# Gate and up products of a transformer block's FFN with the weights as stationary operand

## The chip, the cores and the metric

The kernel runs on one core of a Trainium2 chip. The core has five engines that run side by side and meet at semaphores: TensorE (matrix products), VectorE, ScalarE, GpSimd and SyncE, which issues most of the DMAs. The profile calls them PE, DVE, ACT, POOL and SP, and shows TensorE's weight loads apart from its matmuls, as PEld. The metric is the time of one execution on the device in microseconds, and lower is better. The time before is the median of three runs, 1760.88 us (1760.65 to 1761.78).

## The reference

One block: a mixer of four branches, then an FFN, for 256 tokens of width 2048 in fp32. The change is in the FFN, which is 5632 wide:

```python
def swiglu(h, w_g, w_u, w_d):
    return (jax.nn.silu(h @ w_g) * (h @ w_u)) @ w_d
...
x = x + g1 * merge_branches(h, branches, w_gate[i], w_branch, w_o[i])
x = x + g2 * swiglu(modulate(rms_norm(x, norm2_w[i]), sh2, sc2),
                    w_ffn_gate[i], w_ffn_up[i], w_ffn_down[i])
```

`h` is 256 x 2048, `w_g` and `w_u` are 2048 x 5632, `w_d` is 5632 x 2048.

## The kernel before

A TensorE matmul has a stationary operand (`lhsT`, loaded into the array first, up to 128 columns) and a moving one (`rhs`, streamed through it, up to 512 columns). It sums over the 128 partitions and writes into a bank of PSUM, with one row for each stationary column and one column for each moving one.

**Products in three parts.** Large products are made in the type fp32r. Each fp32 operand is split into a rounded part `hi` and a rest `lo`, and `hi*hi + hi*lo + lo*hi` are summed in PSUM. For weights, `split` (line 76) has ScalarE copy the piece to `hi` (line 94) and VectorE subtract (line 95). Three buffers each of `hi` and `lo` go round. For activations `tsplit` does the same (lines 137 and 138).

**`gemm`** makes 256 tokens by 512 columns of a product. It goes through the contraction in pieces of two k-tiles of 128 rows: one DMA of 512 KB on SyncE's queue, one split, and then for each k-tile and each half `t` of the tokens three matmuls (`mm3`, lines 98 to 101). The activations are stationary (128 features x 128 tokens) and the weights moving (128 x 512), so a PSUM bank holds 128 tokens x 512 columns. With 16 k-tiles (`KT`) that is 16 x 2 x 3 = 96 matmuls. The pools give four PSUM banks to products (`acc`) and four to transposes and small results (`tr`).

**The FFN** (from line 915) goes over eleven groups of 512 columns. For group `n` the gate product goes into `fg` tiles, ScalarE writes its silu to `m` (`mid` in the profile, line 921), the up product goes into `fu` tiles, and VectorE multiplies it into `m` (line 925). `m` has tokens on its partitions. The down product needs features there, so TensorE transposes `m` in eight blocks of 128 x 128, as plain fp32 matmuls with the identity (line 933, `m_tp`), and `tsplit` makes `mh` and `ml` from PSUM. The lists of these, `mT`, are the stationary operand of the down product (`dn` tiles), four groups of 512 columns with 44 k-tiles each, which ends the kernel.

**Order.** Within an engine, instructions run in the order in which they are issued. A scheduler makes that order from the program and its dependencies. It places the transposes of a group a few matmuls into the gate product of the next one, and the last group's into the beginning of the down product. Beside all this, jobs taken from a list (`pump`) accumulate the block's other modulation vectors on VectorE (`macc`) until about the middle of the FFN.

Of the kernel before, what the change touches and what calls it, by code (L numbers as in the profile page):

```python
# [9 lines left out]
F32R = mybir.dt.float32r  # L10
# [5 lines left out]
P = 128  # L16
D = 2048
S = 256
NT = S // P
KT = D // P  # L20
# [26 lines left out]
def block_kernel(ctx: ExitStack, tc: tile.TileContext, t_in, out):  # L47
    nc = tc.nc
# [10 lines left out]
    def U(name, dtype=F32):  # L59
        return up.tile([P, 1024], dtype, tag="u", name=name, bufs=NU)  # L60
# [4 lines left out]
    def acc_ps(name):  # L65
        return psa.tile([P, 512], F32, tag="acc", name=name)

    def tr_ps(name):
        return pst.tile([P, 512], F32, tag="tr", name=name)


    def raw_tile(name):
        return wp.tile([P, 1024], F32, tag="raw", name=name, bufs=NRAW)
# [4 lines left out]
    def split(src, name, shape, roomy=False):  # L78

        n = 1  # L80
        for s_ in shape:
            n *= s_
        assert n <= 1024
        if roomy:
            hi, lo = U(name + "h", F32R), U(name + "l", F32R)
        else:
            hi = wp.tile([P, 1024], F32R, tag="hi", name=name + "h", bufs=3)
            lo = wp.tile([P, 1024], F32R, tag="lo", name=name + "l", bufs=3)
        if len(shape) == 2:
            hv = hi[:, :n].rearrange("p (a b) -> p a b", a=shape[0])  # L90
            lv = lo[:, :n].rearrange("p (a b) -> p a b", a=shape[0])
        else:
            hv, lv = hi[:, :n], lo[:, :n]
        state["act"] = nc.scalar.copy(hv, src)  # L94
        state["dve"] = nc.vector.tensor_tensor(lv, src, hv.bitcast(F32), ALU.subtract)  # L95
        return hv, lv

    def mm3(ps, xh, xl, wh, wl, first, last):
        nc.tensor.matmul(ps, lhsT=xh, rhs=wh, start=first, stop=False)  # L99
        nc.tensor.matmul(ps, lhsT=xh, rhs=wl, start=False, stop=False)  # L100
        state["pe"] = nc.tensor.matmul(ps, lhsT=xl, rhs=wh, start=False, stop=last)  # L101

    def gemm(xT, w, row0, nk, col0, name, tail=1, inside=()):

        pieces = []
        ps = [acc_ps(f"{name}_ps{t}") for t in range(NT)]
        for k0 in range(0, nk, 2):  # L110
            raw = raw_tile(f"{name}_w{k0}")
            rv = raw.rearrange("p (k f) -> p k f", k=2)
            r = row0 + k0 * P
            nc.sync.dma_start(
                rv, w[r:r + 2 * P, col0:col0 + 512].rearrange("(k p) f -> p k f", p=P))
            pump()
            wh, wl = split(rv, f"{name}_{k0}", (2, 512), k0 + 2 * tail >= nk and tail > 1)
            pieces += [(k0 + j, wh[:, j, :], wl[:, j, :]) for j in range(2)]
            next_step()
            if k0 == 4:  # L120
                for do in inside:
                    do()
            if k0 + 2 * tail < nk:
                tiles = [(p_, t) for p_ in pieces for t in range(NT)]
                pieces = []
            elif k0 == nk - 2:
                tiles = [(p_, t) for t in range(NT) for p_ in pieces]
            else:
                continue
            for (kt, h_, l_), t in tiles:  # L130
                xh, xl = xT(kt)
                sl = slice(t * P, (t + 1) * P)
                mm3(ps[t], xh[:, sl], xl[:, sl], h_, l_, kt == 0, kt == nk - 1)
        return ps

    def tsplit(hi, lo, src):
        nc.scalar.copy(hi, src)
        nc.vector.tensor_tensor(lo, src, hi.bitcast(F32), ALU.subtract)
# [5 lines left out]
    state = {"tick": 0, "hold": True}  # L144
# [6 lines left out]
    def pump():  # L151
        state["tick"] += 3
        if state["tick"] >= 5:
            state["tick"] -= 5
            if jobs and not state["hold"]:
                jobs.pop(0)()

    def next_step():
        if steps:
            steps.pop(0)()  # L160
# [16 lines left out]
    ident = const.tile([P, P], F32, name="ident")  # L177
# [598 lines left out]
    for i in range(1, len(CHUNKS) - 1):  # L776
        nk = CHUNKS[i]
# [76 lines left out]
    for n in range(4):  # L854
        while n == 2 and 4 not in col2:
            jobs.pop(0)()
        state["hold"] = n > 1
        ps = gemm(lambda kt: (yT[kt // 4][0][:, kt % 4, :], yT[kt // 4][1][:, kt % 4, :]),
                  t_in["w_o"], 0, KT, n * 512, f"wo{n}", tail=WO_TAIL if n == 3 else 1,
                  inside=wo_later)  # L860
        wo_later = []
        gsl = gbc[2][n // 2][:, (n % 2) * 512:(n % 2) * 512 + 512]
        tmps = U(f"tmp{n}")
        for t in range(NT):
            if n == 3:

                wo_last.append((ps[t], gsl, tmps))
                continue
            wo_later.append(lambda a=(n, t, ps[t], gsl, tmps): residual(*a))
# [7 lines left out]
    def norm2(t):  # L877
        added = residual(3, t, *wo_last[t])
        nc.vector.tensor_reduce(ss2[:, t:t + 1], ssq[:, t, :], AX.X, ALU.add)
        rstd_of(ss2[:, t:t + 1], rs2[:, t:t + 1], 1, 1.0 / D)  # L880
        sl = slice(t * P, (t + 1) * P)
        xns = []
        for q in range(4):
            xn = U(f"xn2_{q}{t}")
            xns.append(xn)
            if q % 2 == 0:
                nc.scalar.activation(xn[:, :512], xres[q][:, t, :], AF.Copy, scale=rs2[:, t:t + 1])
            else:
                nc.vector.tensor_scalar(xn[:, :512], xres[q][:, t, :], rs2[:, t:t + 1], None, ALU.mult)
        for q in range(4):  # L890
            xn, hf = xns[q][:, :512], xns[q][:, 512:]
            ps = tr_ps(f"h2_tp{q}{t}")
            for b in range(4):
                nc.tensor.transpose(ps[:, b * P:(b + 1) * P], xn[:, b * P:(b + 1) * P], ident)
            for b in range(4):
                kt = q * 4 + b
                bs = slice(b * P, (b + 1) * P)
                if b % 2 == 0:
                    nc.vector.tensor_scalar(hf[:, bs], ps[:, bs], a2[:, kt:kt + 1],
                                            col2[3][:, kt:kt + 1], ALU.mult, ALU.add)  # L900
                else:
                    nc.scalar.activation(hf[:, bs], ps[:, bs], AF.Identity, scale=a2[:, kt:kt + 1],
                                         bias=col2[3][:, kt:kt + 1])
            tsplit(h2[q][0][:, :, sl], h2[q][1][:, :, sl], hf.rearrange("p (k t) -> p k t", k=4))
        return added

    with tc.high_priority(offset=NORM2_AHEAD):
        added = norm2(0)
# [5 lines left out]

    mT = []
    for n in range(FF // 512):
        with tc.issue_after(added.ins) if n == 0 else nullcontext():
            pg = gemm(h2x, t_in["w_ffn_gate"], 0, KT, n * 512, f"fg{n}")
        m = U(f"mid{n}").rearrange("p (t f) -> p t f", t=NT)
        for t in range(NT):  # L920
            nc.scalar.activation(m[:, t, :], pg[t], AF.Silu)
        state["hold"] = False
        pu = gemm(h2x, t_in["w_ffn_up"], 0, KT, n * 512, f"fu{n}")
        for t in range(NT):
            nc.vector.tensor_tensor(m[:, t, :], m[:, t, :], pu[t], ALU.mult)
        mh = U(f"mh{n}", F32R).rearrange("p (k t) -> p k t", k=4)
        ml = U(f"ml{n}", F32R).rearrange("p (k t) -> p k t", k=4)
        for pr in range(2):
            ps = tr_ps(f"m_tp{n}{pr}")
            for j in range(2):  # L930
                for t in range(NT):
                    b = pr * 2 + j
                    nc.tensor.transpose(ps[:, (j * 2 + t) * P:(j * 2 + t + 1) * P],
                                        m[:, t, b * P:(b + 1) * P], ident)
            tsplit(mh[:, 2 * pr:2 * pr + 2, :], ml[:, 2 * pr:2 * pr + 2, :],
                   ps.rearrange("p (k t) -> p k t", k=2))
        mT.append((mh, ml))

    while jobs:
# [1 line left out]
    for n in range(4):  # L941
        ps = gemm(lambda kt: (mT[kt // 4][0][:, kt % 4, :], mT[kt // 4][1][:, kt % 4, :]),
                  t_in["w_ffn_down"], 0, FF // P, n * 512, f"dn{n}")
# [78 lines left out]
```

## Time and profile before

The profile shows one execution, with all its instructions on a time axis that starts at the first one.

| | us |
|---|---|
| median of three runs | 1760.88 |
| the profiled execution, on the device | 1761.78 |
| its span on the profile's axis | 1759.7 |
| gate product of group 0 begins | 1019.5 |
| gate product of group 1 begins | 1067.0 |
| down product begins | 1514.0 |

TensorE's matmuls are pipelined, so their spans overlap; how fast it goes is read from the distance of starts. A group row of the profile gives line, engine, operation, output and inputs by the program's names with buffer numbers left out, shapes, count, then busy time, mean ns of one, and the engine's idle time before them with what ended it. In shapes, `128*128 128x512` is a stationary operand of 128 x 128 and a moving one of 128 x 512. Both fp32 and fp32r stand as f32 there: the matmuls of lines 99 to 101 are fp32r, those with `ident`, `s_ps` (attention scores, line 556) and `o_ps` (attention output, line 588) are plain fp32.

### The profile page before, as it was taken

To read this page: it belongs to the slowest core of one execution; us is meant where nothing else is said; L and a number is where in the kernel's file an instruction comes from. 1 tells how busy PE (TensorE), PEld (TensorE's weight loads), DVE (VectorE), ACT (ScalarE), POOL (GpSimd) and SP (SyncE) were. 2 spreads that over 40 slices of the span, in tenths; PEclk is the share of its full clock that TensorE was granted. 3 is DMA by queue.
4 is the path that set the end of the run, shared out by engine and by line. 5 is a ranking of instruction groups with operands and counts; after the bars stand their busy time and mean duration, and the time that the engine had idled before them with its cause. 6 is when DMAs were issued, how large, how long until landed. Compare 5 with 4: busy or idle time off the path is not lost.

```text
span 1759.7 us, 20840 instructions
## 1 busy us (share of the span) xinstructions
PE 1733.2 (98%) x7874; PEld 1396.4 (79%) x7874; DVE 1135.6 (65%) x1302; ACT 742.3 (42%) x874; POOL 56.0 (3%) x74
## 2 busy tenths in 40 slices
PE   6999999999999999999999999999999999999998
PEld 3677777878888888888888878888888888888887
DVE  5875655676588777787878777775554444544554
ACT  5322322344555554444344564445444443433332
POOL 1000000102002000000000000000000000000000
PEclk9999999999999999999999999999999999999999
DMA  9676575446468777999999759875666556565663
GB/s 332 248 287 227 190 250 173 145 124 194 158 200 286 239 247 261 308 306 308 321 323 300 267 172 304 298 252 180 191 189 187 188 190 191 191 202 193 207 206 113
DMA packets 182537, 402.60 MB, mean 229 GB/s; under 512 B 12771, under 2 KB 14997, under 8 KB 182437
## 3 DMA queue, kind: packets, MB, share of 16 engines
q1 hardware_dynamic: 180036, 396.11, 68.0%
q0 software_dynamic: 1248, 3.06, 0.6%
q10 hardware_dynamic: 1152, 2.10, 0.3%
q8 instruction: 62, 1.02, 0.2%
q14 instruction: 39, 0.31, 0.1%
HBM read 399.12 MB, written 2.10 MB: 228 GB/s over the span
## 4 chain that ended last, share of the span: by engine, by line
PE 96%; DMA 1%; DVE 1%; issue 1%; ACT 0%; SPq 0%; POOL 0%; POOLq 0%; DVEq 0%; ACTq 0%
PE gt_ps L100 7%; PE gt_ps L101 7%; PE gt_ps L99 7%; PE in_psx L99 5%; PE in_psx L100 5%; PE fu_ps L100 5%; PE fu_ps L99 5%; PE fu_ps L101 5%; PE in_psx L101 5%; PE dn_ps L101 5%; PE dn_ps L100 5%; PE dn_ps L99 5%; PE fg_ps L99 4%; PE fg_ps L101 4%; PE fg_ps L100 4%; PE br_ps L100 2%
## 5 line engine op out<-in xcount | busy, mean ns | idle before, releaser
L404 DVE SCALAR_TENSOR_TENSOR macc<-mod,cs,macc 128x1024 f32<-128x1024 f32 x128 | 164.0, 1283 | 0.0
L318 DVE TENSOR_TENSOR in_x<-in_x,in_psx 128x512 f32<-128x512 f32 x110 | 74.3, 685 | 45.6 <-PE in_psx L101 45.1
L94 ACT CAST in_2h<-in_w 128x1024 fp32r<-128x1024 f32 x33 | 34.7, 1051 | 160.5 <-PE in_psc L101 91.9
L99 PE MATMUL in_psx<-in_0h,hxh 128*128 128x512 f32 x220 | 90.0, 416 | 1.3 <-ACT hxh L298 1.0
L94 ACT CAST in_0h<-in_w 128x1024 fp32r<-128x1024 f32 (+1 forms) x56 | 57.7, 1035 | 73.0 <-PE in_psx L101 29.1
L100 PE MATMUL in_psx<-in_0l,hxh 128*128 128x512 f32 x220 | 87.2, 399 | 0.0
L101 PE MATMUL in_psx<-in_0h,hxl 128*128 128x512 f32 x220 | 86.3, 395 | 0.0
L95 DVE TENSOR_TENSOR in_0l<-in_w,in_0h 128x1024 fp32r<-128x1024 f32 (+1 forms) x56 | 67.3, 1201 | 3.2 <-ACT in_0h L94 3.2
L95 DVE TENSOR_TENSOR in_2l<-in_w,in_2h 128x1024 fp32r<-128x1024 f32 x33 | 40.4, 1225 | 40.0 <-ACT in_2h L94 40.0
L99 PEld LDWEIGHTS in_psx<-in_0h,hxh 128*128 128x128 f32 x220 | 41.4, 190 | 25.0 <-issue 7.4
L100 PE MATMUL in_psx<-in_2l,hxh 128*128 128x512 f32 x132 | 51.8, 392 | 0.0
L99 PE MATMUL in_psx<-in_2h,hxh 128*128 128x512 f32 x132 | 51.5, 391 | 0.0
L101 PE MATMUL in_psx<-in_2h,hxl 128*128 128x512 f32 x132 | 51.5, 390 | 0.0
L100 PEld LDWEIGHTS in_psx<-in_0l,hxh 128*128 128x128 f32 x220 | 42.1, 191 | 10.8 <-issue 1.9
L101 PEld LDWEIGHTS in_psx<-in_0h,hxl 128*128 128x128 f32 x220 | 41.9, 190 | 9.0
L318 DVE TENSOR_TENSOR in_c<-in_c,in_psc 128x512 f32<-128x512 f32 x40 | 27.2, 686 | 28.6 <-PE in_psc L101 28.5
L226 PE MATMUL mod_ps<-mod_w,cst 128*32 128x512 f32 (+1 forms) x288 | 41.1, 591 | 2.9 <-DMA mod_w<-in_mod 2.8
L95 DVE TENSOR_TENSOR gt_12l<-gt_w,gt_12h 128x1024 fp32r<-128x1024 f32 x16 | 19.6, 1225 | 19.3 <-ACT gt_12h L94 19.3
L99 PE MATMUL in_psc<-in_0h,hch 128*128 128x512 f32 x80 | 31.5, 396 | 0.0
L100 PE MATMUL in_psc<-in_0l,hch 128*128 128x512 f32 x80 | 31.2, 390 | 0.0
L101 PE MATMUL in_psc<-in_0h,hcl 128*128 128x512 f32 x80 | 31.2, 390 | 0.0
L100 PEld LDWEIGHTS in_psx<-in_2l,hxh 128*128 128x128 f32 x132 | 24.8, 188 | 6.0 <-DVE hcl L301 0.8
(659 smaller groups left out, 5132.5 us busy)
## 6 DMA issues: line engine op xcount, KB each, us to landing
mod<-in_w_mod SPq DMA_DIRECT2D x128, 512.0 KB, 5.4
gt_w<-in_w_gate SPq DMA_DIRECT2D x128, 512.0 KB, 5.3
fg_w<-in_w_ffn_gate SPq DMA_DIRECT2D x88, 512.0 KB, 3.6
fu_w<-in_w_ffn_up SPq DMA_DIRECT2D x88, 512.0 KB, 3.6
dn_w<-in_w_ffn_down SPq DMA_DIRECT2D x88, 512.0 KB, 3.8
in_w<-in_w_in SPq DMA_DIRECT2D x87, 512.0 KB, 4.6
mod_w<-in_mod SPq DMA_DIRECT2D x64, 512.0 KB, 5.8
wo_w<-in_w_o SPq DMA_DIRECT2D x32, 512.0 KB, 5.4
```

The source lines that it names most:

```text
L94: state["act"] = nc.scalar.copy(hv, src)
L95: state["dve"] = nc.vector.tensor_tensor(lv, src, hv.bitcast(F32), ALU.subtract)
L99: nc.tensor.matmul(ps, lhsT=xh, rhs=wh, start=first, stop=False)
L100: nc.tensor.matmul(ps, lhsT=xh, rhs=wl, start=False, stop=False)
L101: state["pe"] = nc.tensor.matmul(ps, lhsT=xl, rhs=wh, start=False, stop=last)
L226: nc.tensor.matmul(ps[32 * j:32 * j + 32, :2 * nf], lhsT=cst[:, kk, :], rhs=rvs[j // kn][:, j % kn, :, :].rearrange("p s f -> p (s f)"), s ...
L318: nc.vector.tensor_tensor(dst, dst, ps, ALU.add)
L404: nc.vector.scalar_tensor_tensor(macc[m][h_], mod_raw.pop((m, kk, h_)), cs[:, 0, kk:kk + 1], macc[m][h_], ALU.mult, ALU.add)
```

## The change

A new function `gemm_t` makes the same 256 tokens by 512 columns with the operands' roles swapped: a 128 x 128 block of weights is stationary, and all 256 tokens move. For each k-tile and each of the four blocks `b` of 128 columns there are three matmuls, so 16 x 4 x 3 = 192 in a product. A result has features on its partitions, and two blocks share a PSUM bank: bank 0 holds columns 0 to 255, bank 1 columns 256 to 511, each as two halves of 256 tokens. DMAs, splits and `pump` are as in `gemm`.

In groups 1 to 10 the gate and up products use it. Their `m` then has features on the partitions, so the transposes go, and `tsplit` reads `m` itself in SBUF in place of a transpose's bank. Group 0 stays as it was.

```diff
+    def gemm_t(xT, w, nk, col0, name):
+        ps = [acc_ps(f"{name}_ps{i}") for i in range(2)]
+        for k0 in range(0, nk, 2):
...
+            wh, wl = split(rv, f"{name}_{k0}", (2, 512))
+            next_step()
+            for j in range(2):
+                kt = k0 + j
+                xh, xl = xT(kt)
+                for b in range(4):
+                    sl = slice(b * P, (b + 1) * P)
+                    o = ps[b // 2][:, (b % 2) * S:(b % 2 + 1) * S]
+                    nc.tensor.matmul(o, lhsT=wh[:, j, sl], rhs=xh,
+                                     start=kt == 0 and b % 2 == 0, stop=False)
+                    nc.tensor.matmul(o, lhsT=wh[:, j, sl], rhs=xl, start=False, stop=False)
+                    state["pe"] = nc.tensor.matmul(o, lhsT=wl[:, j, sl], rhs=xh, start=False,
+                                                   stop=kt == nk - 1 and b % 2 == 1)
+        return ps
...
     for n in range(FF // 512):
-        with tc.issue_after(added.ins) if n == 0 else nullcontext():
-            pg = gemm(h2x, t_in["w_ffn_gate"], 0, KT, n * 512, f"fg{n}")
...
+        if n == 0:
+            with tc.issue_after(added.ins):
+                pg = gemm(h2x, t_in["w_ffn_gate"], 0, KT, n * 512, f"fg{n}")
+        else:
+            pg = gemm_t(h2x, t_in["w_ffn_gate"], KT, n * 512, f"fg{n}")
...
         for pr in range(2):
-            ps = tr_ps(f"m_tp{n}{pr}")
-            for j in range(2):
-                for t in range(NT):
-                    b = pr * 2 + j
-                    nc.tensor.transpose(ps[:, (j * 2 + t) * P:(j * 2 + t + 1) * P],
-                                        m[:, t, b * P:(b + 1) * P], ident)
+            if n == 0:
+                src = tr_ps(f"m_tp{n}{pr}")
...
+            else:
+                src = m[:, pr, :]
             tsplit(mh[:, 2 * pr:2 * pr + 2, :], ml[:, 2 * pr:2 * pr + 2, :],
-                   ps.rearrange("p (k t) -> p k t", k=2))
+                   src.rearrange("p (k t) -> p k t", k=2))
```

The up product is switched in the same way as the gate product.

The first place where the order shows it is TensorE's, at the end of group 1's up product (`fu1`) and the start of group 2's gate product (`fg2`). Before, a row being line, operation, output and inputs, and the moving operand's shape:

```order
L101 MATMUL fu1_ps1_8697<-fu1_14h_8841,h2l3_8087 128x512
L99 MATMUL fg2_ps0_8875<-fg2_0h_8879,h2h0_8080 128x512
L100 MATMUL fg2_ps0_8875<-fg2_0l_8880,h2h0_8080 128x512
L933 MATMUL m_tp10_8861<-ident_85,mid1_8693 128x128
L933 MATMUL m_tp11_8868<-ident_85,mid1_8693 128x128
L101 MATMUL fg2_ps0_8875<-fg2_0h_8879,h2l0_8081 128x512
L99 MATMUL fg2_ps1_8876<-fg2_0h_8879,h2h0_8080 128x512
L933 MATMUL m_tp10_8861<-ident_85,mid1_8693 128x128 x3
L933 MATMUL m_tp11_8868<-ident_85,mid1_8693 128x128 x3
L100 MATMUL fg2_ps1_8876<-fg2_0l_8880,h2h0_8080 128x512
```

And in the changed kernel, at the same place:

```order
L160 MATMUL fu1_ps1_8795<-h2h3_8086,fu1_14l_9024 128x256
L157 MATMUL fg2_ps0_9060<-h2h0_8080,fg2_0h_9064 128x256
L159 MATMUL fg2_ps0_9060<-h2l0_8081,fg2_0h_9064 128x256
L160 MATMUL fg2_ps0_9060<-h2h0_8080,fg2_0l_9065 128x256
L157 MATMUL fg2_ps0_9060<-h2h0_8080,fg2_0h_9064 128x256
L159 MATMUL fg2_ps0_9060<-h2l0_8081,fg2_0h_9064 128x256
L160 MATMUL fg2_ps0_9060<-h2h0_8080,fg2_0l_9065 128x256
L157 MATMUL fg2_ps1_9061<-h2h0_8080,fg2_0h_9064 128x256
L159 MATMUL fg2_ps1_9061<-h2l0_8081,fg2_0h_9064 128x256
```

The eight transposes are gone, the moving operands are the activations `h2h` and `h2l` with 256 columns, and `fg2_0h` (the `hi` part of the first piece of weights) is now loaded.

The second place is ScalarE's, where it makes `mh` of group 1 between the splits of group 2's weights. Before:

```order
L94 CAST fg2_2h_8900<-fg2_w2_8895 128x1024
L94 CAST fg2_4h_8921<-fg2_w4_8916 128x1024
L137 CAST mh1_8859<-m_tp10_8861 128x512
L137 CAST mh1_8859<-m_tp11_8868 128x512
L94 CAST fg2_6h_8939<-fg2_w6_8937 128x1024
```

And in the changed kernel:

```order
L94 CAST fg2_2h_9097<-fg2_w2_9092 128x1024
L94 CAST fg2_4h_9130<-fg2_w4_9125 128x1024
L165 CAST mh1_8533<-mid1_8532 128x512 x2
L94 CAST fg2_6h_9160<-fg2_w6_9158 128x1024
L94 CAST fg2_8h_9193<-fg2_w8_9188 128x1024
```

The two copies stand where they stood and read `mid` in place of the transposes' banks. VectorE's subtractions for `ml` keep their place in the same way. SyncE's order of DMAs is the same in both kernels.

More of the change, by code (lines that the diff above doesn't have):

```diff
@@ L133, in gemm @@
                 mm3(ps[t], xh[:, sl], xl[:, sl], h_, l_, kt == 0, kt == nk - 1)
+        return ps
+    def gemm_t(xT, w, nk, col0, name):
+        ps = [acc_ps(f"{name}_ps{i}") for i in range(2)]
+        for k0 in range(0, nk, 2):
+            raw = raw_tile(f"{name}_w{k0}")
+            rv = raw.rearrange("p (k f) -> p k f", k=2)
+            r = k0 * P
+            nc.sync.dma_start(
+                rv, w[r:r + 2 * P, col0:col0 + 512].rearrange("(k p) f -> p k f", p=P))
+            pump()
+            wh, wl = split(rv, f"{name}_{k0}", (2, 512))
[11 more added lines that the diff above has]
+                                                   stop=kt == nk - 1 and b % 2 == 1)
         return ps
@@ L916, in block_kernel @@
     for n in range(FF // 512):
-        with tc.issue_after(added.ins) if n == 0 else nullcontext():
-            pg = gemm(h2x, t_in["w_ffn_gate"], 0, KT, n * 512, f"fg{n}")
         m = U(f"mid{n}").rearrange("p (t f) -> p t f", t=NT)
+        mh = U(f"mh{n}", F32R).rearrange("p (k t) -> p k t", k=4)
+        ml = U(f"ml{n}", F32R).rearrange("p (k t) -> p k t", k=4)
+        if n == 0:
[3 more added lines that the diff above has]
+            pg = gemm_t(h2x, t_in["w_ffn_gate"], KT, n * 512, f"fg{n}")
         for t in range(NT):
@@ L922, in block_kernel @@
         state["hold"] = False
-        pu = gemm(h2x, t_in["w_ffn_up"], 0, KT, n * 512, f"fu{n}")
+        if n == 0:
+            pu = gemm(h2x, t_in["w_ffn_up"], 0, KT, n * 512, f"fu{n}")
+        else:
+            pu = gemm_t(h2x, t_in["w_ffn_up"], KT, n * 512, f"fu{n}")
         for t in range(NT):
             nc.vector.tensor_tensor(m[:, t, :], m[:, t, :], pu[t], ALU.mult)
-        mh = U(f"mh{n}", F32R).rearrange("p (k t) -> p k t", k=4)
-        ml = U(f"ml{n}", F32R).rearrange("p (k t) -> p k t", k=4)
         for pr in range(2):
-            ps = tr_ps(f"m_tp{n}{pr}")
-            for j in range(2):
-                for t in range(NT):
-                    b = pr * 2 + j
-                    nc.tensor.transpose(ps[:, (j * 2 + t) * P:(j * 2 + t + 1) * P],
-                                        m[:, t, b * P:(b + 1) * P], ident)
+            if n == 0:
+                src = tr_ps(f"m_tp{n}{pr}")
+                for j in range(2):
+                    for t in range(NT):
+                        b = pr * 2 + j
+                        nc.tensor.transpose(src[:, (j * 2 + t) * P:(j * 2 + t + 1) * P],
+                                            m[:, t, b * P:(b + 1) * P], ident)
+            else:
+                src = m[:, pr, :]
             tsplit(mh[:, 2 * pr:2 * pr + 2, :], ml[:, 2 * pr:2 * pr + 2, :],
-                   ps.rearrange("p (k t) -> p k t", k=2))
+                   src.rearrange("p (k t) -> p k t", k=2))
         mT.append((mh, ml))
```

## The prediction

> **What bounds the kernel now.** I read the page from the top: busy time first, then the chain that ended last, then the stage that the change touches.
>
> ```profile
> PE 1733.2 (98%) x7874; PEld 1396.4 (79%) x7874; DVE 1135.6 (65%) x1302; ACT 742.3 (42%) x874; POOL 56.0 (3%) x74
> ...
> PE 96%; DMA 1%; DVE 1%; issue 1%; ACT 0%; SPq 0%; POOL 0%; POOLq 0%; DVEq 0%; ACTq 0%
> ```
>
> TensorE carries 96% of the chain, so the end moves with TensorE's own stream and with nothing else. Is that so in the FFN as well? The view of windows, over one up product of group 1 and the gate product before it, says yes: TensorE is never idle, VectorE and ScalarE are.
>
> ```profile
> core 0: us, PE busy (x) PEld busy (x) DVE busy (x) ACT busy (x) POOL busy (x), PEclk, DMA share, GB/s
> ...
> 1134.25:1156.01 21.76, 21.76 (x97) 18.03 (x96) 15.90 (x14) 8.92 (x9) 0.00 (x0) 1.00 0.92 309
> 1111.53:1134.25 22.72, 22.72 (x105) 18.73 (x104) 17.89 (x17) 10.10 (x11) 0.00 (x0) 1.00 0.90 305
> ```
>
> A busy TensorE says little about its pace, because a matmul's span includes its way through the array. The pace is read from starts. The windows' edges are the first matmuls of fu1 (group 1's up product, 1134.25) and of fg2 (1156.01); between them lie 96 matmuls, so **one fp32r matmul of 128x512 takes 21.76 / 96 = 226.7 ns**, start to start, each with its own weight load. The gate product is the same 96 matmuls and took 22.72: 0.96 us more. The difference lies at its beginning, where the eight transposes of the group before are put in. The same place at the last group, where the down product begins, in TensorE's timeline (start, duration):
>
> ```profile
> 1514.19 0.39 PE L100 MATMUL dn_ps<-dn_0l,mh 128*128 128x512 f32 x1
> 1514.41 0.43 PE L933 MATMUL m_tp<-ident,mid 128*128 128x128 f32 x2
> 1514.60 0.48 PE L101 MATMUL dn_ps<-dn_0h,ml 128*128 128x512 f32 x1
> 1514.91 0.40 PE L99 MATMUL dn_ps<-dn_0h,mh 128*128 128x512 f32 x1
> 1515.15 0.82 PE L933 MATMUL m_tp<-ident,mid 128*128 128x128 f32 x6
> 1515.72 0.48 PE L100 MATMUL dn_ps<-dn_0l,mh 128*128 128x512 f32 x1
> 1516.04 0.40 PE L101 MATMUL dn_ps<-dn_0h,ml 128*128 128x512 f32 x1
> ...
> 1518.35 0.39 PE L99 MATMUL dn_ps<-dn_2h,mh 128*128 128x512 f32 x1
> ```
>
> **The change, part by part.**
>
> *The transposes go: a gain.* Eight per group, ten groups. I take the whole surplus of the place they stand in, 0.96 us, which has their 8 x 0.11 us (six of them lie in 0.82 us, one lasts 0.27) and what the turns between the two kinds cost. 10 x 0.96 = **9.6 us off the path**. Group 0 keeps its eight. If only the transposes' own time went, it would be 80 x 0.11 = 8.8.
>
> *The matmuls: same columns, twice the instructions.* Ten groups with two products each are 20 x 96 = 1,920 matmuls of 512 columns; they become 20 x 192 = 3,840 of 256 columns. The old ones cost 20 x 21.76 = 435.2 us. The sum hangs on one number that the trace doesn't have: s, the pace of an fp32r matmul with 256 columns. Each 10 ns of s are 38.4 us. All fp32r matmuls of this kernel have 512 columns. The nearest rows have 128, 256 and 512 columns, but are plain fp32:
>
> ```profile
> L933 PE MATMUL m_tp<-ident,mid x88: 270/273/325, 1067.5 to 1515.7; 128*128 128x128 f32 x88
> ...
> L588 PE MATMUL o_ps<-pT,in_x x32: 377/378/380, 398.4 to 633.2; 128*128 128x256 f32 x32
> ...
> L556 PE MATMUL s_ps<-qf x32: 590/592/593, 376.9 to 612.1; 128*128 128x512 f32 x32
> ...
> 632.56 1.02 PE L588 MATMUL o_ps<-pT,in_x 128*128 128x256 f32 x4
> ```
>
> From 128 to 256 to 512 columns the median grows by 105 and 214 ns: 0.82 to 0.836 ns a column. Four o_ps matmuls lie in 1.02 us and one lasts 0.378, so their pace is 0.642 / 3 = 214 ns, which is 256 x 0.836: plain fp32 has next to no cost per instruction. Take half of that, 0.418 ns, as the array's time for a column of fp32r, and 512 columns are 214 ns. The measured 226.7 has **12.7 ns on top**. Whose are they?
>
> They are not the next weight load's. In the timeline of the loads the transposes' load waited for VectorE and began 0.21 us after the matmul at 1514.19; that matmul still held the array to 1514.41, 0.22 us.
>
> ```profile
> 1514.40 0.20 PEld L933 LDWEIGHTS m_tp<-ident,mid 128*128 128x128 f32 x2 [0.25 <-DVE mid L925]
> ...
> 1515.70 0.19 PEld L100 LDWEIGHTS dn_ps<-dn_0l,mh 128*128 128x128 f32 x1
> 1515.81 0.19 PEld L101 LDWEIGHTS dn_ps<-dn_0h,ml 128*128 128x128 f32 x1
> ```
>
> So they belong to the matmul, and may be a fixed cost of each or a share of each column. The ten steps from the start at 1516.04 to the one at 1518.35 (all of them fp32r matmuls) take 2.31 us, 231 ns each: just after the transposes the same 512 columns carry 17 ns instead of 12.7. A surplus that changes while the columns stay the same looks like a cost of the instruction. I take it as fixed: s = 107.0 + 12.7 = 119.7, say **120 ns**. Then 3,840 x 0.120 = 460.8 us, **25.6 more than before**. With 17 ns it would be 124, 476.2 us and 41 more. As a share of each column, s is 113.3 and nothing is added. From below, s can't be under the 107 of the columns. From above the nearest rows are o_ps's 214 ns (same 256 columns, plain fp32) and 226.7, if a matmul cost the same whatever its width; both double the stage (+386 to +435 us). I go by the fp32r row, which is the nearest in kind.
>
> The Trainium skill speaks of both halves of s. "TensorE: Matmul & The Clock Gate", section "Back-to-back issue gap", has a warm matmul at its columns over 2.4 GHz plus 2.5 ns. The trace disagrees for fp32r: the rule gives 215.8 ns at 512 columns, the row 226.7. By the rule s would be 109.2, and the sum 419.3 us, 15.9 less than before.
>
> *Twice the weight loads.* 1,920 loads come on top, each recorded at 188 ns (o_ps's loads as well as the products'). A load can only stay hidden if it makes room for the next in less than s. The two loads at 1515.70 and 1515.81, both fp32r, start 0.11 us apart, the first beginning while the last transpose runs: a load needs about 110 ns. Under 120 it just fits, with 10 ns to spare; it is priced at nothing for that reason, and this is the thinnest cover here. If it didn't fit and each pair took the recorded 188 ns, the sum would be 3,840 x 0.188 = 721.9, +287 us. The same skill page, section "LDWEIGHTS (loading the stationary operand)", gives 128 columns over 1.2 GHz, 106.7 ns, which agrees with the 0.11.
>
> *New waits.* Weights are now what is loaded, so the load, not the matmul, waits for the split of a piece (ScalarE's copy, VectorE's subtraction); behind a late load TensorE stands. A piece of two k-tiles is 24 matmuls, 2.88 us at s = 120, against 2.72 before. The work for one piece is these two, one after the other:
>
> ```profile
> L94 ACT CAST fu_6h<-fu_w 128x1024 fp32r<-128x1024 f32 x9 | 9.5, 1055 | 11.2 <-PE fu_ps L101 11.2
> ...
> L95 DVE TENSOR_TENSOR fu_6l<-fu_w,fu_6h 128x1024 fp32r<-128x1024 f32 x9 | 11.0, 1224 | 7.6 <-ACT fu_6h L94 7.6
> ```
>
> 1.06 + 1.22 = 2.28 us, and ScalarE idles until TensorE frees a buffer, so the split runs ahead. A faster s of 110 would ask for a piece per 2.64 us, still slower than the split. Cost nothing.
>
> *tsplit from SBUF, PSUM halves, order.* The copies and subtractions of mh and ml keep number and size and lose a wait for TensorE; VectorE and ScalarE have 27% and 59% free in the up window above, so it is nothing either way. Two products of 256 tokens share a bank, a bank is read once per product as before, and the weights' DMAs are the same, in the same order. Nothing.
>
> **Sum.** 1759.7 + 25.6 - 9.6 = 1775.7 for the span. The profiled execution took 1761.78 us, 2.1 above its span, and lies 0.9 above the median of 1760.88. From the median: 1760.9 + 16.0 = **1777 us**, 0.9% slower.
>
> **The rivals.** About 0.2%, 3.5 us, is what a measurement of this kernel tells from no change.
>
> *The surplus goes with the columns* (not slower). s = 113.3, or some 114 to 117 if the load's 110 ns and the few ns before it starts set the pace. The matmuls then cost -0.1 to +14 us, the transposes give 9.6: 1751 to 1765. It decides at s = 115.8, where the added time equals the 9.6 us. For it: in the steady stretch 226.7 is very constant, as a rate would be. Against it: the 231 ns above. I give it 28%, of which 8 lie within 0.2%.
>
> *The surplus goes away with short matmuls*, as plain fp32 rows have none: s = 107 to 109, -17 to -24 us and -9.6: 1727 to 1735. This is also the result by the skill's 2.5 ns. Against it stands that every steady fp32r row has 12.7. 9%.
>
> *The weight load doesn't fit.* Place: each of the 3,840 pairs. If a load that runs beside an fp32r stream takes over 120 ns, s is the load's: 125 ns give +35 net, 188 give +277. Against it is the 0.11; but that load ran beside a transpose, and beside fp32r matmuls, 227 ns apart, a slower one wouldn't have shown. 13%, most of it at 124 to 135 ns: 1792 to 1834.
>
> *Fixed, as forecast*: s of 118 to 124, 1770 to 1792. 50%.
>
> **How the numbers follow.** The forecast is the likeliest case, 1777; its own range is 1770 to 1792. The range given reaches down over the share-of-columns case (1751, and 2 more for what the turns cost) and up to s = 128 (1808), and leaves out the skill's pace (9%) and the worse loads (8%). Faster by over 0.2%: 20 + 9 = 29%. Within: 8%. Slower: 50 + 13 = 63%.
>
> **What would show it.** In the profile after, first of all the distance from the first fg2 to the first fu2 matmul: 23.0 us by the forecast for 192 matmuls, 21.8 if the surplus goes with the columns, 21.0 or less if it goes away. Gate and up products of one group should now take the same time, without the 0.96 us. No m_tp group but that of group 0, x8. If the load is the limit, TensorE's pace will equal the distance between loads, loads will begin later after the start of the matmul ahead, and last longer than 188 ns. TensorE should stay without idle time there, the chain 96% TensorE. The stages before and after the FFN's gate and up products should keep their length; if they don't, or if TensorE waits for VectorE or ScalarE in the FFN, this account is wrong in a way I have not priced.

## The result and the profile after

| | median us | runs | span of the profiled execution |
|---|---|---|---|
| before | 1761.22 (1760.65 to 1761.78) | 4 | 1759.7 |
| changed | 1776.93 (1774.95 to 1777.24) | 4 | 1774.9 |

The ratio is 1.0087 (95% interval 1.0069 to 1.0104): the change makes the kernel slower by 15.7 us, with 1777 forecast. (Corrections to what stands ahead: `split` begins at line 78, and the last `macc` job starts at 1181.6 us, in group 3 of the FFN, not near its middle.)

The page's lines on busy time and on the chain, of the changed kernel:

```profile
PE 1748.6 (99%) x9714; PEld 1489.2 (84%) x9714; DVE 1136.8 (64%) x1302; ACT 742.3 (42%) x874; POOL 56.0 (3%) x74
...
PE 96%; DMA 1%; DVE 1%; issue 1%; ACT 0%; POOL 0%; POOLq 0%; SPq 0%; DVEq 0%; ACTq 0%
```

TensorE has 1,840 matmuls more (3,840 for 1,920, and 80 transposes fewer). VectorE, ScalarE and GpSimd do what they did, and the chain is TensorE's as before. The view of windows, for the up product of group 2 and the gate product before it (columns: stretch, its length, then busy time and count of PE, PEld, DVE, ACT, POOL, the granted clock, DMA share, GB/s):

```profile
1136.85:1159.89 23.04, 23.04 (x195) 23.04 (x193) 16.27 (x14) 8.98 (x10) 0.00 (x0) 1.00 0.88 294
1113.81:1136.85 23.04, 23.04 (x194) 23.04 (x193) 17.51 (x17) 10.14 (x11) 0.00 (x0) 1.00 0.89 296
```

The windows' edges are again first matmuls. (The prediction's two windows are of group 2 as well: group 1's gate product begins at 1067.0, so what it calls fu1, at 1134.25, is fu2, and its fg2, at 1156.01, is fg3. Its figures stand.) Both products now take 23.04 us for 192 matmuls, 120.0 ns each, and the 0.96 us at the gate's beginning are gone. The weight loads (the third busy time) fill the whole window, where they filled 18.03 of 21.76 before. In the timelines of loads and of matmuls (start, duration), at the first weights of that up product:

```profile
1136.73 0.19 PEld L157 LDWEIGHTS fu_ps<-h2h,fu_0h 128*128 128x128 f32 x1
1136.85 0.19 PEld L159 LDWEIGHTS fu_ps<-h2l,fu_0h 128*128 128x128 f32 x1
1136.97 0.19 PEld L160 LDWEIGHTS fu_ps<-h2h,fu_0l 128*128 128x128 f32 x1
...
1136.85 0.28 PE L157 MATMUL fu_ps<-h2h,fu_0h 128*128 128x256 f32 x1
1136.97 0.28 PE L159 MATMUL fu_ps<-h2l,fu_0h 128*128 128x256 f32 x1
1137.09 0.28 PE L160 MATMUL fu_ps<-h2h,fu_0l 128*128 128x256 f32 x1
```

Each load begins as the matmul ahead begins, and its record runs into the next load's. That looks like a limit, and whether it is one is what the experiments had to settle. In TensorE's groups of these stages the idle time before each is 0.0, as in

```profile
L159 PE MATMUL fu_ps<-h2l,fu_0h 128*128 128x256 f32 x80 | 22.6, 283 | 0.0
L160 PEld LDWEIGHTS fu_ps<-h2h,fu_12l 128*128 128x128 f32 x80 | 15.3, 191 | 0.0
```

so no wait took the transposes' place. The transposes that are left, in the view by line:

```profile
L969 PE MATMUL m_tp<-ident,mid x8: 270/272/330, 1067.2 to 1068.5; 128*128 128x128 f32 x8
```

Where the 15.2 us of the spans come from, by the starts of the stages:

| stage | before | changed | difference |
|---|---|---|---|
| to the first matmul of group 1 | 1067.04 | 1066.70 | -0.3 |
| groups 1 to 10 | 446.92 | 463.67 | +16.75 |
| down product to the end | 245.74 | 244.53 | -1.2 |

In groups 1 to 10 the products add 20 x 1.28 = 25.6 us. What is missing to 16.75, 8.85 us, went with nine sets of transposes (9 x 0.96 would be 8.6). The tenth set stood at the start of the down product, which is 1.2 us shorter.

### The profile page after: what moved, and what is told of

Read it like the earlier page. It is cut to its first block, busy times and chain, and to the rows that moved or that the text cites. A ratio compares the mean times of both kernels' runs of the same rounds, so it can differ in the third digit from the quotient of the medians.

```text
span 1774.9 us, 24519 instructions
## 1 busy us (share of the span) xinstructions
PE 1748.6 (99%) x9714; PEld 1489.2 (84%) x9714; DVE 1136.8 (64%) x1302; ACT 742.3 (42%) x874; POOL 56.0 (3%) x74
## 4 chain that ended last, share of the span: by engine, by line
PE 96%; DMA 1%; DVE 1%; issue 1%; ACT 0%; POOL 0%; POOLq 0%; SPq 0%; DVEq 0%; ACTq 0%
PE gt_ps L100 7%; PE gt_ps L101 7%; PE gt_ps L99 6%; PE in_psx L99 5%; PE in_psx L100 5%; PE in_psx L101 4%; PE dn_ps L100 4%; PE dn_ps L99 4%; PE dn_ps L101 4%; PE fg_ps L157 4%; PE fg_ps L159 4%; PE fg_ps L160 4%; PE fu_ps L160 4%; PE fu_ps L157 4%; PE fu_ps L159 4%; PE br_ps L100 2%
```

## The experiments

The forecast rested on two things that the trace before could not show: that the 13 ns which an fp32r matmul takes beyond its columns are a fixed cost of each, and that the weight load is not what sets 120 ns. Four theories stood against each other: "fixed"; "column" (the surplus grows with the width); "roles" (it comes with the weights as stationary operand); "load" (120 ns is a load's own pace). All kernels stood beside runs of the kernel before on the same chip, 1760.95 us in the first four and 1760.81 in the last three.

**The old roles, but two halves (e1).** `cuts` is (0, 256, 512) in groups 1 to 10 and (0, 512) elsewhere.

```diff
-                mm3(ps[t], xh[:, sl], xl[:, sl], h_, l_, kt == 0, kt == nk - 1)
+                parts = list(zip(cuts, cuts[1:]))
+                for n_, (x_, w_) in enumerate(((xh, h_), (xh, l_), (xl, h_))):
+                    for a_, b_ in parts:
+                        state["pe"] = nc.tensor.matmul(
+                            ps[t][:, a_:b_], lhsT=x_[:, sl], rhs=w_[:, a_:b_],
+                            start=kt == 0 and n_ == 0 and a_ == 0,
+                            stop=kt == nk - 1 and n_ == 2 and b_ == 512)
```

> The kernel before, with activations still stationary and the transposes in place; in groups 1 to 10 each gate and up matmul of 512 columns is made as two of 256. Theory 'fixed' (each fp32r matmul carries 13.3 ns, whatever its role or width): a product takes 192 x 120 = 23.04 us instead of 21.76, 25.6 us more in all, 1786.8. Theory 'column' (the surplus is a share of each column): 21.76 a product and 1761. Theory 'roles' (120 ns comes from loading weights, and from loads that wait for the split): 256 columns run at 107 to 110 ns with the old roles, 20.5 to 21.1 us a product, 1737 to 1748. Theory 'load' (120 ns is what a weight load needs before the next can follow): 23.04 us as well.

Measured: 1785.85 us, ratio 1.0143 (1.013 to 1.0156), 24.9 more than before. The windows of an up product and of the gate product before it (group 7):

```profile
1375.37:1398.41 23.04, 23.04 (x195) 23.04 (x193) 10.18 (x9) 8.86 (x9) 0.00 (x0) 1.00 0.61 183
1351.38:1375.37 23.99, 23.99 (x203) 23.91 (x201) 11.88 (x12) 10.05 (x11) 0.00 (x0) 1.00 0.60 176
```

23.04 again, with activations stationary, and the gate product carries its transposes on top (0.95). "Roles" and "column" fall. The price is that of the smaller matmul, whoever is stationary. "Fixed" and "load" both stand.

**No transposes (e2).** `tsplit` reads `m` directly in groups 1 to 10, so this kernel leaves out the turning of `m`.

```diff
-            ps = tr_ps(f"m_tp{n}{pr}")
+            if n:
+                ps = m[:, pr, :]
+            else:
+                ps = tr_ps(f"m_tp{n}{pr}")
...
```

> The kernel before without the transposes of groups 1 to 10; mh and ml are made from m as it is, so the part left out is the turning of m. If the transposes lie on the path with all of their surplus, 10 x 0.96 = 9.6 us go: 1751.6, and the gate products take 21.76 us. If only their own 0.11 us each counts: 8.8, 1752.4. If something else is late where they stood: no change, 1761.

Measured: 1750.87 us, ratio 0.9943 (0.9931 to 0.9955), 10.1 less.

```profile
1308.20:1329.96 21.76, 21.76 (x97) 18.02 (x96) 10.00 (x9) 8.92 (x9) 0.00 (x0) 1.00 0.67 194
1286.44:1308.20 21.76, 21.76 (x97) 18.02 (x96) 11.99 (x12) 10.07 (x11) 0.00 (x0) 1.00 0.65 194
```

Up and gate products are equal at 21.76. The gain is the whole surplus, and nothing else was late there. e1 and e2 together, +24.9 - 10.1 = +14.8, come within 1 us of the change's 15.7.

**Uneven cuts, to find a load's own pace (e3, e6).** Each 512-column matmul is made as 384 + 128 (e3), or as 320 + 192 (e6), with the old roles. After the narrow one the array is free early and waits for the next load.

The cuts of e1, in the call of the gate product (the up product's is the same), for e3 and with 320 for e6:

```diff
-                      cuts=(0, 256, 512) if n else (0, 512))
+                      cuts=(0, 384, 512) if n else (0, 512))
```

> As the first of these, but each 512-column matmul of groups 1 to 10 is made as one of 384 and one of 128 columns. Theory 'fixed': the next start follows a 384-column one after 160 + 13.3 = 173.3 ns; after a 128-column one after 66.7, unless the load of the next is the limit at its 110 ns: 283 ns a pair, 27.2 us a product, 109 us more, 1870. Theory 'column': 170 ns after 384 columns, 280 a pair, 1864. Theory 'load' (a load needs 120): 173.3 and 120, 293 a pair, 1889. A much longer time after the 128-column one (over 150 ns) would mean that fp32r has another price below 256 columns, which none of the three has.

Measured: 1879.34 us, ratio 1.0671 (1.0658 to 1.0685). The window of one up product (group 6) is 27.66 us long, with two transposes at its end (from 1404.31):

```profile
1376.79:1404.45 27.66, 27.66 (x196) 27.66 (x195) 10.40 (x9) 8.87 (x9) 0.00 (x0) 1.00 0.52 153
```

Starts of matmuls mislead here: those of 384 columns are recorded some 50 ns before the next load begins, so they seem to be recorded while they still wait for their weights. I go by the starts of loads, which in steady stretches lie 2 to 3 ns behind the start of the matmul ahead. The timeline of the loads in an up product, two merged in a row:

```profile
1399.95 0.30 PEld L136 LDWEIGHTS fu_ps<-fu_12h,h2h 128*128 128x128 f32 x2
1400.24 0.30 PEld L136 LDWEIGHTS fu_ps<-fu_12l,h2h 128*128 128x128 f32 x2
1400.53 0.30 PEld L136 LDWEIGHTS fu_ps<-fu_12h,h2l 128*128 128x128 f32 x2
```

Two loads lie in 0.30 us and the second lasts 0.19, so they start 0.11 us apart; the pair repeats every 0.287. Over all pairs of groups 1 to 10 the starts of loads lie 108.5 ns apart across the 128-column matmul and 178.2 across the 384-column one. **A load's pace is 108.5 ns, not 120.** "Load" falls; its 293 ns a pair too. "Fixed" had 283, the measured pair has 287: the load takes 1.5 ns less than the 110 expected, and the 384-column matmul that comes after a wait takes 5 ns more than its 173.3.

> The kernel before; each 512-column matmul of groups 1 to 10 made as one of 320 and one of 192 columns. With a load pace of 108.5 ns (seen with 384 and 128) and 13.3 ns fixed, 192 columns (93.3 ns) still fall under the load's pace: 146.7 + 108.5 = 255.2 ns a pair, 24.5 us a product, 1816; with the 5 ns more that the 384-column one showed after a load-bound one, 260 ns, 25.0 us, 1825. If a load beside an fp32r stream needs 120 after all: 267 ns, 25.6 us, 1838. If loads are no limit and only columns and 13.3 count: 240, 23.04 us, 1787.

Measured: 1824.36 us, ratio 1.0362 (1.0341 to 1.0383). An up product (group 6, 1348.47 to 1373.56) takes 25.09 us, with two transposes at its end. The loads in another:

```profile
1400.32 0.30 PEld L136 LDWEIGHTS fu_ps<-fu_0l,h2h 128*128 128x128 f32 x2
1400.58 0.30 PEld L136 LDWEIGHTS fu_ps<-fu_0h,h2l 128*128 128x128 f32 x2
1400.84 0.30 PEld L136 LDWEIGHTS fu_ps<-fu_0h,h2h 128*128 128x128 f32 x2
```

The same picture, repeated every 0.26 us. Again 108.5 ns across the narrow one, 192 columns, and 150.0 across the 320-column one, 3.3 over its line. 258.5 ns a pair, between the two figures that were expected with the 108.5.

**A third width alone (e5).** The cuts again, against e1; the first matmul for each half of the tokens keeps its 512 columns.

```diff
-                    for a_, b_ in parts:
+                    for a_, b_ in ([(0, 512)] if kt == 0 and n_ == 0 else parts):
...
-                      cuts=(0, 256, 512) if n else (0, 512))
+                      cuts=(0, 384) if n else (0, 512))
```

> The kernel before; in groups 1 to 10 all gate and up matmuls but the first for each half of the tokens stream only 384 of their 512 columns, so the last 128 columns of m lack most of their sum (left out). No load is near its limit here, so the third width shows the line. Theory 'fixed': 160 + 13.3 = 173.3 ns a matmul, 16.75 us a product. Theory 'column' (17/16 of the columns' time): 170.0 ns, 16.43 us. In the later groups, where VectorE has no other jobs, TensorE should not wait for the split (2.1 us for a piece); the whole is some 100 us shorter, 1661, and longer if it waits in the first groups.

Measured: 1665.46 us, ratio 0.946 (0.9441 to 0.9479). TensorE's timeline inside an up product:

```profile
1271.13 0.33 PE L136 MATMUL fu_ps<-fu_8h,h2h 128*128 128x384 f32 x1
...
1273.21 0.33 PE L136 MATMUL fu_ps<-fu_10h,h2h 128*128 128x384 f32 x1
```

These are the first matmuls of two pieces, twelve apart: 2.08 / 12 = 173.3 ns. "Column" wanted 170.0, so 2.04 us. In groups 1 to 3 the products took 16.9 to 20.0 us, since pieces came too slowly for that pace. The longest entry in the view of waits of the loads, in groups 2 and 3 (us in total, times, longest):

```profile
PEld fg_ps L136 <- DVE fg_2l L95: 3.1, 2, 1.7
```

With three shorter entries the loads waited 4.7 us there for VectorE's subtraction, about the 4 us over the 1661. The later up products took 16.91, which is the 16.75 and two transposes at their end.

**Fewer matmuls in the new roles (e4, e7).** In groups 4 to 10 a function `gemm_w` stands in place of `gemm_t`. In it hi and lo of the activations move past the weights' hi in one matmul of 512 columns, and hi alone past the weights' lo; each block has a PSUM bank of its own, and VectorE adds its two halves afterwards. Of `gemm_w`, against the changed kernel:

```diff
+                both = h2_of[0][kt // 2][:, kt % 2, :, :]
+                for b in range(4):
+                    sl = slice(b * P, (b + 1) * P)
+                    nc.tensor.matmul(ps[b], lhsT=wh[:, j, sl], rhs=both.rearrange("p s t -> p (s t)"),
+                                     start=kt == 0, stop=False)
+                    state["pe"] = nc.tensor.matmul(ps[b][:, :S], lhsT=wl[:, j, sl], rhs=both[:, 0, :],
+                                                   start=False, stop=kt == nk - 1)
...
```

> The changed kernel; in groups 4 to 10 hi and lo of the activations move together as one operand of 512 columns past a block of weights' hi, into two halves of a bank, and only hi moves past the weights' lo: two matmuls (512 and 256 columns) in place of three of 256, the same columns, each product in four banks, with the halves added by VectorE afterwards. h2 is kept in pairs for that, with 8 more short copies and 8 more subtractions before the FFN. Theory 'fixed': a product takes 64 x (226.7 + 120) = 22.19 us instead of 23.04, 14 x 0.85 = 11.9 us less, and up to 1 us more before the FFN: 1765 to 1766. Theory 'roles': with weights stationary the 512-column matmul takes more than 226.7, and less than 11.9 is won. Theory 'column' gives no change, 1777.

Measured: span 1762.9, 12.0 under the changed kernel's.

```profile
1318.56:1340.75 22.19, 22.19 (x131) 19.57 (x129) 12.36 (x17) 9.80 (x12) 0.00 (x0) 1.00 0.65 189
1296.37:1318.56 22.19, 22.19 (x130) 19.57 (x129) 14.73 (x23) 9.57 (x10) 0.00 (x0) 1.00 0.63 190
```

64 x (226.7 + 120) = 22.19, as expected: a third of the matmuls less, the same columns, 0.85 us less. By time it is not so clean: the median was 1768.63, ratio 1.0046 (1.0033 to 1.0059) to the kernel before, and the single times lie at 1765 and at 1771. The same kernel once more:

> The kernel with hi and lo moving together once more, since its runs lay at 1765 and at 1771. If the 6 us are in the products or before the FFN, a profile of a longer run shows which stage is longer; the theories expect 22.19 us a product in groups 4 to 10 either way.

Measured: 1767.93, ratio 1.0048 (1.003 to 1.0067). Of ten runs in both series five lie at 1764.7 to 1766.3 and five at 1770.6 to 1771.9. Both profiles are of executions of the first kind, with the same 22.19; where the others lose 6 us stays open.

No version that does all of the work lies below the kernel before. With all ten groups made like e4 the sum would be 1776.9 - 20 x 0.85 = 1759.9, 1.3 us under it and less than a measurement tells; it wasn't run.

## Why the prediction was right

| step | forecast | measured |
|---|---|---|
| pace of an fp32r matmul with 256 columns | 120 ns | 120.0 ns |
| matmuls | +25.6 us | +25.6 (20 x 1.28), e1 +24.9 in time |
| transposes | -9.6 us | -8.85 in groups 2 to 10 and -1.2 in the down product; e2 -10.1 in time |
| weight loads | hidden, 10 ns to spare | hidden, pace 108.5 ns |
| waits, `tsplit`, order | 0 | TensorE has no idle time in the products |
| sum | +16.0 us | +15.7 (spans: +15.2) |

**The pace** was the one unknown, and the number came out. The line now has three widths without a wait: 120.0, 173.3 and 226.7 ns for 256, 384 and 512 columns, which is **0.4167 ns a column and 13.3 ns for each matmul**. Two steps on the way to it were weaker than they read, and there luck had a part.

The 0.418 ns a column was half of the 0.836 of the plain fp32 rows, and no row said why half. What is more, the "four o_ps matmuls" are four records of two matmuls: line 588 issues 32 matmuls (eight heads, four each) and the trace has 64 records, so 0.836 is the price of a record, not of a plain fp32 matmul. That half of it is the array's time for fp32r is shown only by the three widths above.

The choice of "fixed" over "column" was made on the 231 ns after the transposes. They do not show it. In the changed kernel no transpose stands before the down product, and its first steps are as long:

```profile
1530.37 0.40 PE L99 MATMUL dn_ps<-dn_0h,mh 128*128 128x512 f32 x1
...
1531.53 0.39 PE L101 MATMUL dn_ps<-dn_0h,ml 128*128 128x512 f32 x1
...
1532.89 0.39 PE L101 MATMUL dn_ps<-dn_0h,ml 128*128 128x512 f32 x1
```

Five steps take 1.16 us, 232 ns each, and the next six 1.36, 226.7 each. In e2, where 512-column matmuls stand before the down product, its first ten steps take 2.27 us, 227 each. So the longer steps come behind a stretch of narrower matmuls, transposes or not, and are gone after some steps; they say nothing on how the 12.7 ns go with the width. "Fixed" was right, as e1 and e5 show, but not for the reason that was given. Why those steps are longer stays open.

One thing is also not shown: whose the 13.3 ns are. Every matmul in these runs has a weight load of its own, so the price is that of a matmul and its load together. That the matmul at 1514.19 held the array for its 0.22 us with no other load beside it speaks against the next load's time, but not against a cost of changing the weights. The records of plain fp32 matmuls have a load each as well and next to nothing on top (214 ns for 256 columns). No run here has a matmul that keeps its weights.

The Trainium skill ("TensorE: Matmul & The Clock Gate", section "Back-to-back issue gap") has the slope, since 0.4167 is one column at 2.4 GHz, but adds 2.5 ns, for a single matmul by itself, in place of the 13.3, and by it the change would have come out faster. For fp32r the runs decide: 13.3.

**The cover over the loads** held, by 11.5 ns. One sign that I named for "the load is the limit" did appear all the same: most loads of these products last 192 ns in place of 188, and the loads' row is full. Another did not: loads still begin 2 to 3 ns after the start of the matmul ahead. The first sign was a poor one. A load's record is longer than the pace at which loads follow each other, so records of neighbours overlap and a full row comes at any pace under 190 ns. Only the uneven cuts told the two apart.

**The rivals.** "The surplus goes with the columns" falls with e1 and e5, "it goes away with short matmuls" with e1, "the load doesn't fit" with e3 and e6, for 256 columns.

## What to carry to other kernels

When a change keeps the columns streamed through TensorE but cuts them into more matmuls, count matmuls: here each fp32r one, with a weight load of its own, costs 13.3 ns beyond its columns, and 1,920 more of them cost 25.6 us, against 9.6 us for the 80 transposes that they replaced. By these figures, widths under (108.5 - 13.3) / 0.4167 = 228 columns fall under the load's pace and cost more still; 192 and 128 columns did. And to learn whether loads or matmuls set a pace, don't read how full the loads' row is; make one matmul of a pair so short that a load has to be waited for, and measure from load to load.

## What the runs showed that was not expected

The load's pace and the matmul's at 256 columns are only 11.5 ns apart, so this change sat near the edge of a much dearer case: at 384 + 128 columns an up product took 27.66 us (two transposes in it), where one of 512-column matmuls takes 21.76. And a matmul that follows one which waited for its weights takes 3 to 5 ns more than its line (150.0 for 146.7, 178.2 for 173.3); no run here says why.
